# A hybrid attention, state-space and expert-retrieval block: low halves of gated tiles moved to ScalarE, low parts of expert blocks moved to VectorE, and a new order of issue

## The chip, the cores and the metric

The kernel runs on one core of a Trainium2 chip. The metric is the device time of one execution in microseconds; the median of several runs is compared. All engine times below are from one profiled execution.

## The reference

The input is a sequence of 512 tokens of width 1024, ahead of which 16 learned tokens are put. One layer is computed:

```python
proj = rms_norm(h, norm1_g) @ w_in
attn = sliding_window_attention(q, k, v)         # window 128, 8 query heads, 2 key heads, sinks
ssm  = s5_ssm(u)                                 # 32 groups, 64 complex states, then gelu and a gate
h = h + concat(rms_norm(attn), rms_norm(ssm)) @ w_out
# expert retrieval, 8 heads, on hc = rms_norm(h, norm2_g):
s1, s2 = q[..., :128] @ keys1.T, q[..., 128:] @ keys2.T          # q = hc @ w_query
sc, idx = top 16 of the sums of the top 16 of s1 and the top 16 of s2
act = gelu(hc @ u[idx]) * softmax(sc)
h = h + sum over the 16 picks of act * v[idx]    # 16384 experts, u and v are 16384 x 1024
```

## The kernel before, in words

**Mixer** (`front`): projections, state space, attention and the output product, up to the normalized activations hT, which lie transposed in SBUF as a high part hTh and a low part hTl. Products are taken in three passes, high by high, low by high and high by low; `split` makes the two parts of an operand (ScalarE rounds, VectorE subtracts). Its steps are written out in the table STEPS by name: Lx and Sx load and split x, Lwu, Lwq and Lwkv load weights and Swu, Swq, Swkv split them, u and q are the products with them, rot and co are GpSimd's rotations and output weights of the state space, and wt (L173, a helper that records every such operation) are its input weights on VectorE.

**Query and gate stages** (`body`, up to the end of the table WSTEPS). Steps, again by name:

- Lq, Aq, Dq, qm, qk, qs, qo: a block of w_query is loaded, rounded by ScalarE (Aq), its low part is subtracted (Dq, class `Query`, `lo`), multiplied and scored against the keys. tk and tp take the top 16; ca, ga, gx, gn, rk, xe and oh pick keys and gates of 128 tokens (class `Pick`).
- Lu, Au, Du, sm, so, each with a number b: an expert block of 128 experts is loaded into ur, rounded into uh on ScalarE, its low part ul is subtracted (`u_lo`), 24 matmuls give the scores of 384 tokens (`s_mm`), and ScalarE takes gelu (`s_out`). 51 blocks are done here ahead of the expert stage, in this order: by the table. ul and uh have two buffers each, and the query's parts share them.
- Class `Gates`: for the first three groups n of 128 tokens the gates are spread into a matrix over 128 x 128 experts. A tile holds 8 tokens: go makes the one-hot rows of both keys (goh), gg multiplies the second key's rows by the gate (ggt; the gate has a high half, elements 0 to 3 of the tile, and a low half, 4 to 7, both float16), gm multiplies the two on TensorE, four tokens at a time, gc copies the result into gst, and gs stores 16 tokens in DRAM. goh and ggt have two buffers each.
- rl and rs gather and use rows for the last 128 tokens, whose picks are fetched by themselves.

What is issued is a plain list: each step is recorded when its name comes up, and each engine runs its own instructions in that order. An instruction that waits holds up all that stand behind it on its engine. The names are in the tables; nothing else orders them.

**Expert stage** (the loop at the end of `body`): all gates are loaded from DRAM in turns (gc), and for each of 128 blocks the scores are multiplied by them (L1470), split (ph, pl) and multiplied with v (acc, 18 matmuls of 512 columns). For the blocks that were not done ahead, the steps of an expert block run there too, with the low part on VectorE.

The lines that the change touches:

```python
def gated(self, u):                                   # gg: both halves by VectorE
    ...
        self.nc.vector.tensor_tensor(g[:, qs], self.oh[u][:, 4:8], self.row(self.g2, u)[:, qs], op=ALU.mult)
(self.nc.vector if self.ct < 2 else self.nc.gpsimd).tensor_tensor(self.l, ...)          # Query.lo
(nc.gpsimd if b < AHEAD and b % LO[1] < LO[0] else V).tensor_tensor(lo, ...)            # u_lo, LO = (1, 1)
```

so that all 51 low parts of the blocks done ahead are GpSimd's, and of the query's 16 the first two VectorE's.

Of the kernel before, what the change touches and what calls it, by code (L numbers as in the profile page):

```python
# [1548 lines left out]
```

## Time and profile before

| | |
|---|---|
| time of three runs, median (lowest to highest) | 1556.37 us (1556.08 to 1556.42) |
| the profiled execution's own time, and its span | 1555.96 us, 1554.2 us |
| TensorE matmul busy, granted clock over the span | 1465.4 us (94%), 0.969 |
| TensorE weight load busy | 1293.8 us (83%) |
| VectorE busy | 1240.7 us (80%) |
| ScalarE busy | 639.9 us (41%) |
| GpSimd busy | 633.2 us (41%) |
| chain that ended last | TensorE 73%, VectorE 22% |

Busy time is the union of an engine's instructions as profiled; a matmul's end is modelled. The span is the time from the first to the last instruction. Idle time of an engine that is not the bound costs nothing. [...]

### The profile page before, as it was taken

How to read it: one execution, taken by the hardware profiler on the slowest of the kernel's cores; microseconds unless marked ns; L12 is line 12 of the kernel's file. 1: busy time of each engine (PE TensorE's matmuls, PEld its weight loads, DVE VectorE, ACT ScalarE, POOL GpSimd, SP SyncE). 2: the span in 40 equal slices, each digit the busy share in tenths (PEclk: the TensorE clock that was granted, in tenths of full speed). 3: DMA queues.
4: the chain of work that ended last, by engine and by line, in shares of the span. 5: the costliest groups of instructions: out<-in, count | busy, mean ns of one | idle time of the engine just before them, and what ended most of it. 6: DMA issues, size and time to landing. Idle time of an engine off the chain costs nothing.

```text
span 1554.2 us, 22068 instructions
## 1 busy us (share of the span) xinstructions
PE 1465.4 (94%) x8062; PEld 1293.8 (83%) x8062; DVE 1240.7 (80%) x2296; ACT 639.9 (41%) x995; POOL 633.2 (41%) x419
## 2 busy tenths in 40 slices
PE   7789898999788887999999999999999999999998
PEld 7667586889687787998879999999999999999886
DVE  8977934769999998847778887788878888778776
ACT  5235823334457665643333333333333333333332
POOL 6841210334454444552334444344434444344330
PEclk9779998999899898999999999999999999999999
DMA  6162116232456465786889999898998989999874
GB/s 235 59 93 75 62 41 239 92 112 76 144 188 234 158 232 184 255 314 216 291 300 351 327 356 349 314 327 304 339 318 311 344 290 344 311 318 335 307 271 149
DMA packets 161053, 371.60 MB, mean 239 GB/s; under 512 B 19872, under 2 KB 79008, under 8 KB 157744
## 3 DMA queue, kind: packets, MB, share of 16 engines
q1 hardware_dynamic: 123504, 234.90, 44.2%
q0 software_dynamic: 36864, 134.23, 24.5%
q8 instruction: 63, 1.03, 0.3%
q10 hardware_dynamic: 576, 1.05, 0.2%
q14 instruction: 46, 0.38, 0.1%
HBM read 330.91 MB, written 38.04 MB: 237 GB/s over the span
## 4 chain that ended last, share of the span: by engine, by line
PE 73%; DVE 22%; issue 2%; ACT 2%; DMA 1%; POOL 0%; SPq 0%; DVEq 0%; ACTq 0%
PE acc L1516 11%; PE acc L1517 11%; PE acc L1515 11%; PE ps_sb L1307 8%; PE ps_sb L1309 8%; PE ps_sb L1308 8%; DVE ggt L1190 5%; DVE goh L1180 3%; PE ps_qq L1045 2%; PE ps_qq L1046 2%; PE ps_qq L1047 2%; DVE wt L173 2%; DVE oh L1138 1%; PE ps_wo L186 1%; PE ps_wo L187 1%
## 5 line engine op out<-in xcount | busy, mean ns | idle before, releaser
L1307 PE MATMUL ps_sb<-hTh,uh 128*128 128x384 f32 x1024 | 353.4, 345 | 1.9 <-ACT uh L1295 1.9
L1309 PE MATMUL ps_sb<-hTh,ul 128*128 128x384 f32 x1024 | 348.3, 340 | 6.2 <-POOL ul L1299 5.5
L1308 PE MATMUL ps_sb<-hTl,uh 128*128 128x384 f32 x1024 | 346.8, 339 | 0.0
L1515 PE MATMUL acc<-vh,ph 128*128 128x512 f32 x768 | 299.5, 390 | 3.3 <-ACT ph L94 3.3
L1517 PE MATMUL acc<-vh,pl 128*128 128x512 f32 x768 | 301.3, 392 | 0.0
L1516 PE MATMUL acc<-vl,ph 128*128 128x512 f32 x768 | 301.0, 392 | 0.0
L1340 POOL DMA_INDIRECT row_grow<-in_v_rows_dram,idx x128 | 181.1, 1415 | 246.2 <-DVE ac L1367 194.9
L1340 POOL DMA_INDIRECT row_grow<-in_u_rows_dram,idx x116 | 158.1, 1363 | 249.9 <-DVE dots L1360 211.1
L1299 POOL TENSOR_TENSOR ul<-ur,uh 128x1024 fp32r<-128x1024 f32 x51 | 144.5, 2836 | 163.7 <-ACT uh L1295 163.5
L95 DVE TENSOR_TENSOR vl<-vr,vh 128x1024 fp32r<-128x1024 f32 x128 | 156.8, 1225 | 61.4 <-ACT vh L94 57.1
L1309 PEld LDWEIGHTS ps_sb<-hTh,ul 128*128 128x128 f32 x1024 | 194.9, 190 | 8.8 <-POOL ul L1299 7.8
L1307 PEld LDWEIGHTS ps_sb<-hTh,uh 128*128 128x128 f32 x1024 | 195.7, 191 | 5.6 <-ACT uh L1295 2.6
L1308 PEld LDWEIGHTS ps_sb<-hTl,uh 128*128 128x128 f32 x1024 | 195.7, 191 | 2.9
L1315 ACT ACTIVATE s<-ps_sb 128x384 f32<-128x384 f32 x128 | 63.0, 494 | 302.4 <-PE ps_sb L1309 299.2
L1367 DVE SCALAR_TENSOR_TENSOR ac<-row_grow,dots,ac 128x1024 f32<-128x1024 f32 x128 | 164.2, 1283 | 9.9 <-DMA row_grow<-in_v_rows_dram,idx 7.5
L1515 PEld LDWEIGHTS acc<-vh,ph 128*128 128x128 f32 x768 | 144.8, 189 | 32.2 <-ACT ph L94 3.9
L1517 PEld LDWEIGHTS acc<-vh,pl 128*128 128x128 f32 x768 | 144.5, 188 | 31.0 <-DVE pl L95 0.6
L1516 PEld LDWEIGHTS acc<-vl,ph 128*128 128x128 f32 x768 | 144.3, 188 | 28.4
L94 ACT CAST vh<-vr 128x1024 fp32r<-128x1024 f32 x128 | 134.0, 1047 | 40.3 <-PE acc L1517 38.4
L1295 ACT CAST uh<-ur 128x1024 fp32r<-128x1024 f32 x128 | 134.2, 1049 | 28.9 <-PE ps_sb L1308 9.6
L1360 DVE CUSTOM_DVE_ANT_0 row_grow<-row_grow,hcr 128x1024 f32<-128x1024 f32 x116 | 137.4, 1220 | 1.2 <-DMA row_grow<-in_u_rows_dram,idx 0.9
L94 ACT CAST ph<-s 128x384 fp32r<-128x384 f32 x100 | 51.4, 514 | 189.8 <-DVE s L1470 189.8
(338 smaller groups left out, 2331.4 us busy)
## 6 DMA issues: line engine op xcount, KB each, us to landing
ur<-in_uT_dram SPq DMA_DIRECT2D x128, 512.0 KB
vr<-in_v_dram SPq DMA_DIRECT2D x128, 512.0 KB
gates<-gst SPq DMA_DIRECT2D x24, 1024.0 KB
gc<-gates SPq DMA_DIRECT2D x16, 1536.0 KB
wqr<-in_w_query_dram SPq DMA_DIRECT2D x16, 512.0 KB
s_spill<-s SPq DMA_DIRECT2D x28, 192.0 KB
sr<-s_spill SPq DMA_DIRECT2D x28, 192.0 KB
wor<-in_w_out_dram SPq DMA_DIRECT2D x16, 256.0 KB
```

Source lines behind the costliest of these rows:

```text
L94: nc.scalar.copy(hi, src)
L95: (eng or nc.vector).tensor_tensor(lo, src, hi.bitcast(F32), op=ALU.subtract)
L1299: (nc.gpsimd if b < AHEAD and b % LO[1] < LO[0] else V).tensor_tensor(lo, ur.pop(b), hs[b].bitcast(F32), op=ALU.subtract)
L1307: E.matmul(p, hi[:, k], hTh[k][:, :384], start=(k == 0), stop=False)
L1308: E.matmul(p, hi[:, k], hTl[k][:, :384], start=False, stop=False)
L1309: E.matmul(p, lo[:, k], hTh[k][:, :384], start=False, stop=(k == KD - 1))
L1340: nc.gpsimd.indirect_dma_start(out=t, out_offset=None, in_=table, in_offset=bass.IndirectOffsetOnAxis(ap=idx[:, k:k + 1], axis=0))
L1360: V.tensor_tensor_reduce(t, t, hcr, 1.0, 0.0, op0=ALU.mult, op1=ALU.add, accum_out=dots[:, k:k + 1])
L1367: V.scalar_tensor_tensor(ac3, t, dots[:, k:k + 1], ac3, op0=ALU.mult, op1=ALU.add)
L1515: E.matmul(acc[n][h], ph[:, ts], vh[:, cs], start=(b == 0), stop=False)
L1516: E.matmul(acc[n][h], ph[:, ts], vl[:, cs], start=False, stop=False)
L1517: E.matmul(acc[n][h], pl[:, ts], vh[:, cs], start=False, stop=(b == 127))
```

## The change

It is in four parts. The new tables STEPS and WSTEPS hold the same steps as before in another order, and WSTEPS has new ones, gl. For the odd tiles u of each group (24 of 48), gg makes the high half alone, and gl makes the low half on ScalarE: two groups of four copies with a scale by partition, one copy for a token, reading and writing every second float16. The scale is the low part of the gate in float32 (gl). 28 of the 51 early low parts go to VectorE (the set UV), 23 remain on GpSimd. Of the query's low parts, VectorE has 0 and 7 in place of 0 and 1. The rest of the diff lets tiles be allocated in the new order (dictionaries in place of lists, views made only where they are used).

```diff
 STEPS = """
-    ang Lx0 Sx0 Lwu0 Lwu1 Swu0 Lwu3 Lwu4 sin Lwkv1 u0 Lx2 Lprm rot0 Swu3 Lx4 Sx1 par0 Swu1 par1 Swu4 par2 rot1
...
+    bdz Lx4 drz Lwu3 Lwu1 ang Lwu5 Lx0 Swu3 Sx4 Lwu0 Lwu4 Swu1 sin par0 Lprm Swu0 Sx1 Lwu6 Lwq0 par1 Sx0 Swu5 Lwkv3
...
+    wc01 q0 k1 wt20 us0 kv2 us3 wt21 Swq1 kvc0 we21 wt30 co20 wc11 kvc4 kvc1 q1 wt31 ui0 ui1 M0z kc1 we20 we31 we30
...
-        (self.nc.vector if self.ct < 2 else self.nc.gpsimd).tensor_tensor(self.l, self.raw, self.h.bitcast(F32), op=ALU.subtract)
+        (self.nc.vector if self.ct in QV else self.nc.gpsimd).tensor_tensor(self.l, self.raw, self.h.bitcast(F32), op=ALU.subtract)
...
+        self.gl = GP.tile([128, 128], F32, name=f"gl{n}", tag="gl", bufs=2)
         g8 = gT.rearrange("p (u t) -> p u t", t=8)
-        V.tensor_copy(self.g2[:, :, 0], g8)
-        V.tensor_tensor(self.g2[:, :, 1], g8, self.g2[:, :, 0], op=ALU.subtract)
+        V.tensor_copy(self.g2[:, 0], g8)
+        V.tensor_tensor(self.gl.rearrange("p (u t) -> p u t", t=8), g8, self.g2[:, 0], op=ALU.subtract)
+        V.tensor_copy(self.g2[:, 1], self.gl.rearrange("p (u t) -> p u t", t=8))
...
     def gated(self, u):
-        self.g[u] = g = self.GP.tile([128, 8, 128, 2], F16, name="ggt", tag="ggt", bufs=2)
-        for x in range(2):
-            qs = slice(4 * x, 4 * x + 4)
-            self.nc.vector.tensor_tensor(g[:, qs], self.oh[u][:, 4:8], self.row(self.g2, u)[:, qs], op=ALU.mult)
+        for x in range(1 if u in LA[self.n] else 2):
+            self.nc.vector.tensor_tensor(self.out(u)[:, 4 * x:4 * x + 4], self.oh[u][:, 4:8],
+                                         self.row(self.g2[:, x, u], 4), op=ALU.mult)
+
+    def gated_low(self, u, q):
+        oh, g = self.oh[u], self.out(u)
+        for x in range(4 * q, 4 * q + 4):
+            y, s = divmod(x, 2)
+            t = u * 8 + x
+            self.nc.scalar.activation(g[:, 4 + y, :, s], oh[:, 4 + y, :, s], AF.Copy, scale=self.gl[:, t:t + 1])
...
+QV = {0, 7}
+LA = [{u for u in range(16) if u % 2}] * 3
+UV = {0, 2, 4, 5, 6, 8, 10, 11, 15, 16, 17, 19, 20, 22, 29, 32, 36, 37, 38, 39, 40, 41, 43, 46, 47, 48, 49, 50}
...
-    gc2.7.0 sm8 gc2.7.1 Lu9 gc2.6.1 so8 gs2.3 Au12 sm17 so17 Du12 Au9 sm12 rl11 Au7 Du9 Du7 Lu18 sm9 so12 Au18 so9
-    sm7 Du18 so7 rs11 sm18 so18
+    gc2.15.0 gg2.6 gs2.6 so17 Du12 gn3 gc2.14.0 rs9 gc2.7.0 rl7 gm2.7.1 gm2.6.1 rs7 gc2.7.1 Lu18 gm2.6.0 gs2.7 gc2.6.1
+    Au7 Du9 gc2.6.0 sm12 sm9 Du7 so12 rs10 rl8 so9 Au18 Du18 gs2.3 sm7 sm18 so7 so18 rs8
 """
...
-            (nc.gpsimd if b < AHEAD and b % LO[1] < LO[0] else V).tensor_tensor(lo, ur.pop(b), hs[b].bitcast(F32),
+            (nc.gpsimd if b < AHEAD and b not in UV else V).tensor_tensor(lo, ur.pop(b), hs[b].bitcast(F32),
                                                                                 op=ALU.subtract)
...
+                            if u in LA[n]:
+                                step(f"gl{n}.{u}.{q}", g.gated_low, u, q)
                             step(f"gm{n}.{u}.{q}", g.mm, u, q)
```

How it stands in the order, at two places. VectorE, the first gated tiles of the first group of tokens, before (goh one-hot, ggt gated; a line of x2 is the two halves of one tile):

```order
L1180 TENSOR_TENSOR goh_4133<-itx_2502,iT0_4122 128x2048
L1190 TENSOR_TENSOR ggt_4163<-goh_4133,g20_4126 128x1024 x2
L1180 TENSOR_TENSOR goh_4166<-itx_2502,iT0_4122 128x2048
L1432 SCALAR_TENSOR_TENSOR idx_2485<-i1_2482,i2_2483 128x128
L1190 TENSOR_TENSOR ggt_4195<-goh_4166,g20_4126 128x1024 x2
```

and now, on VectorE:

```order
L1182 TENSOR_TENSOR goh_4217<-itx_2502,iT0_4130 128x2048
L1196 TENSOR_TENSOR ggt_4219<-goh_4217,g20_4134 128x1024
L1182 TENSOR_TENSOR goh_4221<-itx_2502,iT0_4130 128x2048
L1196 TENSOR_TENSOR ggt_4258<-goh_4221,g20_4134 128x1024 x2
L1319 TENSOR_TENSOR ul38_4261<-ur38_3259,uh38_4202 128x1024
```

An odd tile has one VectorE operation in place of two, and a low part (ul38) stands among them.

ScalarE, at the end of the gate stage, before (gst copies gate results from PSUM, uh rounds an expert block, s is gelu of a block's scores, vh belongs to the expert stage):

```order
L1295 CAST uh17_6664<-ur17_6629 128x1024
L1205 COPY gst_6647<-ps_gm_6677 128x4x128
L1205 COPY gst_6647<-ps_gm_6666 128x4x128
L1205 COPY gst_6647<-ps_gm_6649 128x4x128
L1315 ACTIVATE s8_6716<-ps_sb8_6687 128x384
L1295 CAST uh12_6719<-ur12_6598 128x1024
L1315 ACTIVATE s17_6746<-ps_sb17_6721 128x384
L1295 CAST uh9_6750<-ur9_6713 128x1024
L94 CAST vh0_6899<-vr0_6893 128x1024
L1295 CAST uh7_6779<-ur7_6662 128x1024
```

and now:

```order
L1315 CAST uh9_6869<-ur9_6687 128x1024
L1219 COPY gst_6718<-ps_gm_6725 128x4x128
L1335 ACTIVATE s17_6878<-ps_sb17_6830 128x384
L1219 COPY gst_6718<-ps_gm_6807 128x4x128
L1219 COPY gst_6888<-ps_gm_6855 128x4x128
L1219 COPY gst_6888<-ps_gm_6892 128x4x128
L1219 COPY gst_6888<-ps_gm_6901 128x4x128
L1315 CAST uh7_6925<-ur7_6871 128x1024
L1219 COPY gst_6888<-ps_gm_6914 128x4x128
L1335 ACTIVATE s12_6982<-ps_sb12_6930 128x384
```

The last copy of gates now stands behind uh7 and ahead of blocks 12, 9, 7 and 18; before, it stood ahead of blocks 8, 17, 12, 9, 7 and 18. uh7 takes the buffer of uh12, two roundings back, which block 12's matmuls read; on TensorE these stand behind the last gate matmul.

## Rows read from the trace of the kernel before

**Rows 1.** Busy time of each engine in stretches of the execution: the stretch in us from the span's start, its length, then for PE, PEld (weight loads), DVE, ACT and POOL the busy us and the count of instructions, the granted clock, the busy share of the DMA engines, and GB/s.

```profile
0.00:256.70 256.70, 222.54 (x1397) 175.99 (x1397) 198.95 (x404) 116.89 (x312) 98.69 (x98) 0.92 0.39 107
...
41.00:129.00 88.00, 75.87 (x519) 58.68 (x520) 75.69 (x103) 28.01 (x62) 50.85 (x33) 0.81 0.46 87
...
250.00:275.00 25.00, 20.21 (x81) 16.49 (x82) 10.84 (x46) 8.07 (x22) 5.00 (x3) 0.80 0.66 231
...
256.70:369.90 113.20, 112.47 (x550) 95.06 (x551) 77.29 (x516) 35.59 (x50) 39.63 (x17) 0.98 0.31 107
...
300.00:325.00 25.00, 25.00 (x126) 21.05 (x125) 18.06 (x124) 8.37 (x12) 9.45 (x5) 1.00 0.28 95
...
369.90:666.60 296.70, 252.37 (x1808) 240.50 (x1807) 279.64 (x545) 173.45 (x206) 142.55 (x55) 0.93 0.56 198
```

**Rows 2.** Who waited for whom, TensorE in 369.9 to 694.2 us: the instruction and what ended the wait, us in total, times, the longest.

```profile
PE ps_gm L1199 <- DVE ggt L1190: 14.8, 17, 2.9
...
PE ps_gm L1198 <- DVE ggt L1190: 12.6, 11, 2.8
```

**Rows 3.** The same for ScalarE in 369.9 to 666.6 us.

```profile
ACT s L1315 <- PE ps_sb L1309: 37.7, 17, 5.8
...
ACT gst L1205 <- PE ps_gm L1199: 35.9, 16, 7.1
```

**Rows 4.** Groups of VectorE's instructions of one shape in 369.9 to 666.6 us: line, operation, out<-in, shape, count | busy us, mean ns of one | idle us just before them and what ended it.

```profile
L1190 DVE TENSOR_TENSOR ggt<-goh,g 128x1024 f16<-128x1024 f16 x96 | 100.3, 1093 | 0.8
...
L1180 DVE TENSOR_TENSOR goh<-itx,iT 128x2048 f16<-128x2048 f16 x48 | 63.1, 1330 | 12.0 <-PE ps_gm L1199 12.0
...
L1132 DVE TENSOR_TENSOR oh<-it,rk 128x2048 f16<-128x2048 f16 x8 | 14.8, 1847 | 0.1
...
L1135 DVE TENSOR_TENSOR oh<-oh,xe 128x2048 f16<-128x2048 f16 x8 | 13.8, 1720 | 0.4
...
L1138 DVE TENSOR_TENSOR oh<-oh 128x1024 f16<-128x1024 f16 x8 | 11.8, 1474 | 0.2
```

**Rows 5.** Single operations on VectorE over the whole execution: duration in ns, shortest/median/longest, first and last start.

```profile
L1190 DVE TENSOR_TENSOR ggt<-goh,g x96: 674/685/3232, 429.1 to 665.8; 128x1024 f16<-128x1024 f16 x96
...
L1180 DVE TENSOR_TENSOR goh<-itx,iT x48: 1203/1217/3443, 427.8 to 654.3; 128x2048 f16<-128x2048 f16 x48
...
L1299 DVE TENSOR_TENSOR ul<-ur,uh x77: 1220/1226/1227, 813.0 to 1438.9; 128x1024 fp32r<-128x1024 f32 x77
```

**Rows 6.** VectorE in order of time: start us, us, engine, line, operation, out<-in, shape, count. Both handle 128 integers.

```profile
449.82 2.28 DVE L1111 TENSOR_SCALAR tci<-tci 128x128 uint32<-128x128 uint32 x1
...
454.39 0.21 DVE L1115 CAST tc<-tci 128x128 f32<-128x128 uint32 x1
```

**Rows 7.** GpSimd in order of time, the same columns, and the idle time before with what ended it.

```profile
446.35 8.03 POOL L1299 TENSOR_TENSOR ul<-ur,uh 128x1024 fp32r<-128x1024 f32 x2 [6.83 <-ACT uh L1295]
```

**Rows 8.** GpSimd's group of low parts in 369.9 to 666.6 us, columns as in rows 4.

```profile
L1299 POOL TENSOR_TENSOR ul<-ur,uh 128x1024 fp32r<-128x1024 f32 x44 | 127.5, 2902 | 149.3 <-ACT uh L1295 149.2
```

**Rows 9.** ScalarE in order of time in the mixer; L448 is a copy of 128 x 128 from SBUF with a scale by partition, and the second row is the instruction right behind it.

```profile
47.91 0.39 ACT L448 ACTIVATE dg<-ident,r 128x128 f32<-128x128 f32 x1
...
48.20 0.39 ACT L587 COPY bdr<-prm 64x256 f32<-64x256 f32 x1
```

**Rows 10.** Groups of ScalarE's instructions of one shape in 240 to 860 us, columns as in rows 4; ACT_TABLE_LOAD loads the table of an activation function.

```profile
L1205 ACT COPY gst<-ps_gm 128x512 f32<-128x512 f32 x96 | 92.9, 1096 | 41.7 <-PE ps_gm L1199 35.9 <-issue 5.6
...
L1052 ACT COPY qqT<-ps_qq 128x512 f32<-128x512 f32 x16 | 9.4, 585 | 39.7 <-PE ps_qq L1047 39.7
...
L1315 ACT ACT_TABLE_LOAD x4 | 5.1, 1283 | 0.1
```

**Rows 11.** ScalarE in order of time at the hand-over, with the idle time before and what ended it; a row of L1315 follows the end of one block's 24 matmuls, L1295 is a rounding uh.

```profile
667.95 2.86 ACT L1205 COPY gst<-ps_gm 128x512 f32<-128x512 f32 x3
...
671.85 0.49 ACT L1315 ACTIVATE s<-ps_sb 128x384 f32<-128x384 f32 x1 [1.04 <-PE ps_sb L1309]
...
672.23 1.04 ACT L1295 CAST uh<-ur 128x1024 fp32r<-128x1024 f32 x1
...
676.05 0.49 ACT L1315 ACTIVATE s<-ps_sb 128x384 f32<-128x384 f32 x1 [2.77 <-PE ps_sb L1309]
```

**Rows 12.** TensorE in order of time: the first of the last 32 gate matmuls (four groups), the first matmul behind them, and the first of the expert stage.

```profile
665.09 0.23 PE L1198 MATMUL ps_gm<-ggt,goh 128*128 128x128 f16 x1
...
667.36 0.42 PE L1307 MATMUL ps_sb<-hTh,uh 128*128 128x384 f32 x1
...
694.14 0.39 PE L1515 MATMUL acc<-vh,ph 128*128 128x512 f32 x1
```

**Rows 13.** VectorE's waits in 369.9 to 666.6 us, columns as in rows 2.

```profile
DVE goh L1180 <- PE ps_gm L1199: 12.0, 6, 3.1
```

**Rows 14.** DMA issues on SyncE's queue, in order of time: the last store of gates and the first load.

```profile
670.83 0.33 SPq L1209 DMA_DIRECT2D gates<-gst  x1
...
676.20 0.38 SPq L1460 DMA_DIRECT2D gc<-gates  x1
```

**Rows 15.** VectorE in order of time at the hand-over: the product of scores and gates of block 0, and the low part pl made from it.

```profile
688.80 1.38 DVE L1470 SCALAR_TENSOR_TENSOR s<-gc,s 128x384 f32<-128x384 f32 x1 [1.30 <-DMA gc<-gates]
...
690.75 0.56 DVE L95 TENSOR_TENSOR pl<-s,ph 128x384 fp32r<-128x384 f32 x1 [0.58 <-ACT ph L94]
```

**Rows 16.** One kind of the mixer's wt on VectorE, columns as in rows 5.

```profile
L173 DVE TENSOR_TENSOR wt<-prm,pr x8: 667/1796/1919, 41.2 to 80.9; 128x512 f32<-128x512 f32 x8
```

More of the change, by code (lines that the diff above doesn't have):

```diff
@@ L317, in params @@
         def params(i):
-            prm = t["prm"]
-            b_re, b_im, c_re, c_im, bbr, bbi, tb1, tb2 = (prm[:, x] for x in range(8))
+            if i >= 4:
+                b_re, b_im, c_re, c_im, bbr, bbi, tb1, tb2 = (t["prm"][:, x] for x in range(8))
             if i == 0:
@@ new lines, in row, with out @@
+    def row(self, z, n):
+        return z.rearrange("p (q s) -> p q s", s=2)[:, :, None].to_broadcast([128, n, 128, 2])
+    def out(self, u):
+        if u not in self.g:
+            self.g[u] = self.GP.tile([128, 8, 128, 2], F16, name="ggt", tag="ggt", bufs=2)
+        return self.g[u]
+    def gated(self, u):
+        for x in range(1 if u in LA[self.n] else 2):
+            self.nc.vector.tensor_tensor(self.out(u)[:, 4 * x:4 * x + 4], self.oh[u][:, 4:8],
+                                         self.row(self.g2[:, x, u], 4), op=ALU.mult)
@@ L1201, in copy @@
     def copy(self, u, q):
-        if u % 2 == 0 and q == 0:
+        if u // 2 not in self.st:
             self.st[u // 2] = self.GP.tile([128, 128, TS], F32, name="gst", tag="gst", bufs=2)
@@ new lines @@
+    oh2.1.3 go1.12 oh2.1.4 go1.13 gl1.15.0 gl1.15.1 so0 gc1.5.1 gc1.4.0 gg1.12 Lu20 gm1.14.0 gm1.15.1 gs1.3 so3 Au6
+    gm1.14.1 oh2.1.5 gc1.14.0 Du6 gm1.15.0 sm4 go1.10 gc1.4.1 gm1.12.0 gl1.13.0 gs1.2 gc1.15.0 gt2 gg1.13 Lu14 gp2
+    Lu13 gc1.15.1 gg1.10 gm1.12.1 Au11 Du11 sm6 gc1.14.1 gm1.13.0 gl1.13.1 go2.0 gc1.12.1 so6 gc1.13.0 gm1.13.1
+    gc1.13.1 go2.1 gs1.7 gg2.0 gc1.12.0 gm1.10.1 gm1.10.0 so4 gg2.1 gs1.6 go1.11 go2.5 Au13 gl2.1.1 sm11 gg1.11
+    gm2.1.1 gg2.5 gm2.0.1 gm2.0.0 Au14 gl2.1.0 go2.4 Du13 gm2.1.0 rl6 gc2.1.1 gl1.11.0 go2.2 gl2.5.1 gc2.0.0 sm13
@@ new lines @@
+    gl2.5.0 gg2.4 Du14 Lu10 gc2.0.1 gg2.2 gc1.10.1 Lu19 Lu5 gl1.11.1 so13 gm2.5.1 gc2.1.0 so11 gm2.5.0 gm1.11.0
+    gm1.11.1 sm14 Au20 gm2.4.0 gc1.11.0 gc1.11.1 Du20 go2.8 gs2.0 gc1.10.0 so14 gc2.5.0 Au10 gm2.4.1 Lu16 rs6 go2.9
+    gg2.8 gm2.2.0 Du10 gc2.4.0 go2.3 gm2.2.1 gc2.5.1 sm20 gl2.9.0 gg2.9 gc2.4.1 Lu22 rl4 rl5 Au16 so20 gl2.9.1 gm2.8.1
+    gs1.5 gl2.3.0 Au5 rl3 gm2.8.0 sm10 gg2.3 gs2.2 Du16 gm2.9.0 gm2.9.1 go2.10 so10 gc2.8.1 gc2.9.0 Lu21 Du5 gc2.8.0
+    Au19 sm16 gg2.10 rs4 rl11 Lu2 gm2.10.1 Du19 so16 gc2.9.1 gm2.10.0 go2.11 gm2.3.0 gl2.3.1 gl2.11.1 gl2.11.0 rs3
@@ new lines @@
+    gg2.11 Au21 gs2.4 gc2.2.0 sm5 gm2.3.1 gc2.2.1 go2.13 sm19 so5 gl2.13.1 go2.12 gg2.13 gc2.3.0 gm2.11.1 Au2 rs5
+    gg2.12 gc2.3.1 Du21 gm2.11.0 gc2.11.1 Du2 go2.15 so19 Lu15 sm21 Au15 Du15 gm2.13.1 gc2.10.0 gm2.12.0 so21 gg2.15
+    gc2.10.1 gm2.12.1 gc2.11.0 Au22 rs11 sm2 Lu8 sm15 gl2.13.0 gl2.15.0 gl2.15.1 so2 Du22 Lu17 Lu9 gc2.13.1 go2.14
+    gs2.1 gm2.13.0 Au8 gm2.15.1 gg2.14 gc2.13.0 gc2.15.1 gs2.5 so15 Du8 gm2.15.0 go2.7 rl9 gl2.7.1 Au17 Lu12 sm22
+    gc2.12.1 rl10 so22 gc2.12.0 sm8 gl2.7.0 gm2.14.0 Au12 Du17 gg2.7 gm2.14.1 sm17 gm2.7.0 gc2.14.1 so8 go2.6 Au9 Lu7
```

138 lines of the change are left out of this document (61 added, 77 removed).

## The prediction

> **What bounds the kernel now.** I read the page's engine totals first, then busy times by stretch, then who waited for whom in the stretch that the change is about, then single operations there. The stretches [rows 1]: mixer 0 to 257 us, query stage 257 to 370, gate stage 370 to 667 (from the first candidate sums, ca3, to the last gated tile, gg2.6), hand-over 667 to 694, and expert stage from 694 to the end, where TensorE is full. The gate stage is 296.7 us long and VectorE is busy for 279.6 of it; TensorE is busy for 252.4 at a granted clock of 0.93, ScalarE for 173.5. So VectorE sets the pace there: TensorE's largest waits are 27.4 us for gated tiles [rows 2]. ScalarE is often idle there, for PE's results (37.7 and 35.9 us) [rows 3].
>
> VectorE's own operations are not at one length. A gated half has a median of 685 ns and a mean of 1093; a one-hot tile 1217 and 1330 [rows 4, 5]. The long ones stand beside GpSimd's subtractions: two of these ran in 446 to 454 us, and a shift of 128 integers took 2.28 us there where a conversion of as many took 0.21 right after [rows 6, 7]. A GpSimd subtraction thus stops VectorE for about 2 us. Over the stage, mean minus median of like operations is 39 us for 96 gated halves, 5 for 48 one-hots, 9 for 16 oh of 2048 (L1132, L1135, against the one-hot's 1217) and 6 for 8 oh of 1024 (against 685): 60 us in these forms alone beside 44 subtractions [rows 4, 5, 8], so 1.4 us for one at least; the single case says 2.1. I take 1.8.
>
> **The change, part by part.** *Low parts of 28 blocks on VectorE.* Of the 44 GpSimd subtractions in the gate stage 18 are left. VectorE gains 26 x 1.8 = 47 us of waits and pays 28 x 1.226 us (its own time for this operation [rows 5]) = 34 us: net -13 us. With 1.4 it is -2, with 2.1 it is -21. The query's two on VectorE remain two (0 and 7 for 0 and 1), at nothing: TensorE is full in that stage [rows 1].
>
> *Low halves of the odd tiles on ScalarE.* 24 of 96 gated halves leave VectorE, 24 x 0.685 = -16 us. ScalarE gets 192 scaled copies of 128 x 128. The nearest rows are the mixer's dg, the same form from SBUF with a scale by partition: 0.39 to 0.40 us long, 0.29 to 0.31 from one start to the next [rows 9]. 192 x 0.31 = 60 us. No row shows a copy whose elements lie 4 bytes apart on both sides. ScalarE's gst copy, which writes with a step, takes 1.096 us for 512 elements, while qqT, packed, takes 0.585 [rows 10]: 1.87 times as long for as many, so the upper end is 0.58 and the lower 0.29. I take 0.31, the nearer form. Two more table loads stand in the new order, 1.28 us each [rows 10].
>
> [...]
>
> *Gate stage.* VectorE: 279.6 - 16 - 13 = 250. ScalarE: 173.5 + 60 + 3 = 236. TensorE at full clock: 46 blocks of 4.2 us (one result each 4.20 us [rows 11]) and 93 groups of gate matmuls of 0.5 (32 matmuls, four groups, in 2.3 us [rows 12]), 240 (before, 44 blocks: 232). VectorE remains the longest, but the three now lie within 14 us, each in a fixed order, and each odd tile has one more station (VectorE, ScalarE, TensorE), held up by whatever ScalarE waits for. Before, the stage was VectorE's 280 + 17, of which 12.0 us were waits for gate matmuls to free a one-hot buffer [rows 13]. I put the new idle time at 22 us: stage 272, a gain of 25. The bounds: 250 + 10 = 260 where less stalling also gives TensorE its clock back, and 290 where ScalarE's waits (123 us idle before) shrink by little more than half: 236 + 54.
>
> *Hand-over.* Before, the last gate matmul ended at 667.4, the last gst copies at 670.8, the store went out at 670.8, the load of gates at 676.2, VectorE had them at 688.8 and ph and pl by 691.3; TensorE was busy with six blocks until 694.1 and never waited for them [rows 11, 12, 14, 15]. In the new order four blocks (12, 9, 7, 18) stand behind the last gate matmul, 16.8 us. And the last gst copy stands behind uh7 on ScalarE, whose buffer is free only when block 12's matmuls are done: 4.2 + 1.04 + 0.95 us after the last gate matmul, 6.2 instead of 3.4 [rows 11, 12]. From there the chain is as before, 691.3 - 670.8 = 20.5. So the first expert matmul starts 26.7 us after the last gate matmul, about 28 us after the last gated tile, and TensorE stands idle for 10 us. Before it was 27.6 after the last gated tile, so this costs 0.5, and the clock after the pause more: where TensorE stood idle for 4.8 us in 250 to 275, the clock was 0.80 for those 25 us [rows 1]. That is 10 us at the lower level, at most 5 us of work; I take 3. Together +3.5. Lower end 0; upper 8, where the load is late too.
>
> *Mixer.* No work is added there; the loads and the splits of w_u, the transposes wt, and q0 and q1 change places. Two q steps (24 matmuls at 25.0 / 126 = 0.20 us [rows 1], 4.8 us) move from behind the last wt to ahead of it, where TensorE has room. But wt itself is held by GpSimd: of its 24 operations the eight of one kind have a median of 1.80 us and a shortest of 0.67 [rows 16], and GpSimd is busy for 50.9 of the 88 us between 41 and 129 [rows 1]. The order moves that, it doesn't remove it. I take -3, from -12 to +8: the first w_u product now has to wait for more loads and splits, with VectorE as the bound (75.7 of 88 us between 41 and 129 [rows 1]).
>
> *Expert stage.* Untouched, 694 to 1554.
>
> **Sum**, against the profiled execution's own 1555.96 us (0.4 below the median of the runs, 1556.37): -25 + 3.5 - 3 = -24.5, so 1531.5; with the 0.4 for the median, 1532.
>
> **The rivals.**
> 1. *The freed VectorE time is mostly not used.* TensorE and ScalarE, in fixed orders, become the bound, and the stage ends at 285: 1532 + 13 = 1545. For it: three engines within 14 us of each other. Against it: before, VectorE was idle for only 17 us of 297 and TensorE and ScalarE followed it. Chance 0.22.
> 2. *More than forecast.* A subtraction is worth 2.1 us, and with fewer stalls TensorE keeps its clock: stage 255 to 260, mixer -6: 1514. For it: the single case of 2.1 us, and the clock of 0.93. Chance 0.20.
> 3. *ScalarE becomes the bound, slower than before.* The price of one scaled copy decides. ScalarE's stage is 176 + 192 p plus the idle time of a pacing engine, 17 to 20 us as VectorE had. At p = 0.53 us that is 297, the old length. At the upper end, 0.58, it is 307: 1532 + 35 = 1567. [...] Against it: dg's 0.31, and that gst's step is 64 bytes and not 4. Chance 0.08.
> 4. *VectorE's long operations are not GpSimd's doing*, or GpSimd's row gathers cost the same; then the 34 us are added and only 16 leave: 1556 + 18 + 1 = 1575. The shift of 2.28 us speaks against it [rows 6, 7]. Chance 0.03.
>
> **How the numbers follow.** The forecast has 0.47, its own range 1521 to 1543. The range reaches from 1511 (rival 2) to 1554 (rival 1 with a late hand-over). A measurement of this kernel can tell about 0.2% from no change: 1553.3 to 1559.5. Rivals 3 and 4 lie above (slower 0.11); of rival 1, 0.04 lies within, a stage of 290 with a mixer that loses; the rest is faster, 0.85.
>
> **What would show it.** Right: the gate stage at about 272 us, VectorE busy 250 and gated halves with a mean below 0.95 us; 18 GpSimd subtractions in it; scaled copies 0.4 us long, ScalarE busy about 236; a pause of 10 us of TensorE ahead of the first expert matmul, with a granted clock below 1 behind it; mixer and query within a few us of 370. Wrong: scaled copies above 0.5 us, one-hots waiting far more than 12 us for gate matmuls, a mixer longer by 8 us or more.

## The result, and the profile after

The changed kernel takes 1522.38 us (median of 4 runs, 1521.88 to 1522.85), the kernel before, beside it, 1556.39 (1556.08 to 1558.8): a ratio of 0.9778, 95% interval 0.9761 to 0.9795, 34 us faster. The forecast was 1532, range 1511 to 1554. The profiled execution of the changed kernel took 1522.77 us, its span is 1520.7.

The page's engine totals of the changed kernel, busy us, share of the span and instructions:

```profile
PE 1453.0 (96%) x8062; PEld 1285.6 (85%) x8062; DVE 1188.1 (78%) x2303; ACT 692.9 (46%) x1189; POOL 545.1 (36%) x391
```

Its stretches, cut at the same events as those of before [rows 1], columns as there: mixer, query stage, gate stage, hand-over, and the first 25 us from the first acc matmul.

```profile
0.00:254.00 254.00, 218.89 (x1397) 175.67 (x1398) 189.16 (x403) 115.18 (x311) 97.95 (x98) 0.94 0.38 106
254.00:367.10 113.10, 112.42 (x550) 94.36 (x551) 80.29 (x517) 36.35 (x51) 39.68 (x17) 0.98 0.34 112
367.10:627.87 260.77, 248.00 (x1849) 237.53 (x1848) 231.96 (x545) 228.04 (x401) 60.26 (x29) 0.98 0.64 222
627.87:656.10 28.23, 18.24 (x120) 17.91 (x117) 9.27 (x13) 11.61 (x16) 13.31 (x9) 0.91 0.91 328
656.10:681.10 25.00, 24.98 (x99) 20.43 (x100) 13.56 (x19) 8.87 (x11) 0.36 (x1) 0.89 0.64 217
```

Against the spans of before, 1554.2 - 1520.7 = 33.5 us, stretch by stretch:

| us | before | forecast | after |
|---|---|---|---|
| mixer | 256.7 | -3 | 254.0 (-2.7) |
| query stage | 113.2 | 0 | 113.1 (-0.1) |
| gate stage | 296.7 | -25 | 260.8 (-35.9) |
| hand-over | 27.5 | +0.5 | 28.2 (+0.7) |
| expert stage, to the end of the span | 860.1 | +3 | 864.6 (+4.5) |

So nearly all of the surprise is in the gate stage. There TensorE is now the longest, 248.0 of 260.8 at a granted clock of 0.98 (the share of TensorE's full speed that was granted), ScalarE follows with 228.0, and VectorE has gone from 279.6 to 232.0. VectorE's and GpSimd's groups there that answer to [rows 4] and [rows 8], columns as there:

```profile
L1196 DVE TENSOR_TENSOR ggt<-goh,g 128x1024 f16<-128x1024 f16 x72 | 53.1, 777 | 0.3
L1182 DVE TENSOR_TENSOR goh<-itx,iT 128x2048 f16<-128x2048 f16 x48 | 58.0, 1224 | 21.0 <-PE ps_gm L1213 20.8
L1135 DVE TENSOR_TENSOR oh<-oh,xe 128x2048 f16<-128x2048 f16 x8 | 9.8, 1220 | 0.2
L1132 DVE TENSOR_TENSOR oh<-it,rk 128x2048 f16<-128x2048 f16 x8 | 9.8, 1220 | 0.1
L1319 DVE TENSOR_TENSOR ul<-ur,uh 128x1024 fp32r<-128x1024 f32 x28 | 34.2, 1220 | 5.7 <-ACT uh L1315 5.7
L1319 POOL TENSOR_TENSOR ul<-ur,uh 128x1024 fp32r<-128x1024 f32 x18 | 44.3, 2463 | 103.8 <-ACT uh L1315 75.9 <-DVE ggt L1196 27.9
```

The forms that were long are short: a gated half has a mean of 777 ns instead of 1093, an oh of 2048 elements 1220 instead of 1847. I summed, over all VectorE operations of the gate stage, what each took beyond the shortest of its line and names: 84.3 us before, 21.6 after, so 62.7 us less. The forecast had 47.

Part of this is the 26 subtractions that left; the rest is where the others stand. Experiment 4 gives the new order alone, with all 43 that begin in the stage still on GpSimd, 67.8 us in place of 84.3. GpSimd and VectorE in order of time, changed kernel, first at 391.9 us and then at 624.3 us:

```profile
391.90 4.72 POOL L1319 TENSOR_TENSOR ul<-ur,uh 128x1024 fp32r<-128x1024 f32 x2 [4.82 <-ACT uh L1315]
```

```profile
392.02 0.23 DVE L1015 MATCH_REPLACE8 cand<-tsc,cand 128x80 f32<-128x80 f32 x1
...
392.38 0.38 DVE L1017 MAX8 tsc<-cand 128x8 f32<-128x80 f32 x2
...
392.73 0.23 DVE L1019 FIND_INDEX8 tci<-tsc,cand 128x8 uint32<-128x80 f32 x1
...
624.38 3.49 DVE L1196 TENSOR_TENSOR ggt<-goh,g 128x1024 f16<-128x1024 f16 x2
```

```profile
624.31 2.41 POOL L1319 TENSOR_TENSOR ul<-ur,uh 128x1024 fp32r<-128x1024 f32 x1 [5.88 <-ACT uh L1315]
```

The top-16 operations (MAX8, FIND_INDEX8, MATCH_REPLACE8) take 0.23 us, or 0.38 for two in a row, beside two subtractions, as elsewhere in this execution (medians of 0.23 to 0.24 us over 32 of each, none above 0.25); the pair of gated halves beside the last one takes 3.49 us instead of 1.3. A subtraction thus costs VectorE about 2.2 us where an operation of two tiles begins beside it (1.9 to 2.2 in five places of this stage; 0.3 to 0.9 us in three places where the first such operation begins late in it), and 0.1 to 0.2 us where only the top-16's stand beside it. An operation with one tile as input was not always free: before the change the shift of [rows 6] (2.28 us, where the median of its four is 0.23), and the conversion right behind it (2.45 us, median 0.22), ran beside the two subtractions of [rows 7] and were held up as well:

```profile
452.02 2.45 DVE L1114 CAST tr<-ri 128x128 f32<-128x128 uint32 x1
```

The hand-over of the changed kernel, rows that answer to [rows 11, 12, 14, 15]: ScalarE's last copy of gates, the load of gates on SyncE's queue, VectorE's first product and TensorE's first matmul of the expert stage.

```profile
634.33 1.05 ACT L1219 COPY gst<-ps_gm 128x512 f32<-128x512 f32 x1
```

```profile
641.12 0.37 SPq L1482 DMA_DIRECT2D gc<-gates  x1
```

```profile
654.97 0.56 DVE L1492 SCALAR_TENSOR_TENSOR s<-gc,s 128x384 f32<-128x384 f32 x1 [8.30 <-DMA gc<-gates]
```

```profile
656.12 0.79 PE L1537 MATMUL acc<-vh,ph 128*128 128x512 f32 x1 [10.02 <-ACT ph L94]
```

TensorE's pause is 10.02 us, the chain from the last copy (635.4) to the first matmul 20.7 us, and the granted clock over the next 25 us is 0.89, all three about as forecast.

### The profile page after: what moved, and what is told of

It reads as the page before. It is cut to its first block, busy times and chain, and to the rows that moved or that the text cites. A ratio compares the mean times of both kernels' runs of the same rounds, so it can differ in the third digit from the quotient of the medians.

```text
span 1520.7 us, 22245 instructions
## 1 busy us (share of the span) xinstructions
PE 1453.0 (96%) x8062; PEld 1285.6 (85%) x8062; DVE 1188.1 (78%) x2303; ACT 692.9 (46%) x1189; POOL 545.1 (36%) x391
## 4 chain that ended last, share of the span: by engine, by line
PE 71%; issue 8%; POOL 6%; ACT 6%; DVE 5%; DMA 3%; SPq 1%; POOLq 0%; ACTq 0%; DVEq 0%
PE acc L1537 9%; PE acc L1538 9%; PE acc L1539 9%; PE ps_sb L1327 9%; PE ps_sb L1329 8%; PE ps_sb L1328 8%; POOL row_grow L1360 2%; POOL ptmp L172 2%; PE ps_qq L1045 2%; PE ps_qq L1047 2%; PE ps_qq L1046 2%; ACT gst L1219 2%; ACT ggt L1204 1%; DMA row_grow<-in_v_rows_dram,idx 1%; ACT uh L1315 1%
## 5 line engine op out<-in xcount | busy, mean ns | idle before, releaser
L1360 POOL DMA_INDIRECT row_grow<-in_v_rows_dram,idx x128 | 180.4, 1410 | 248.0 <-DVE ac L1387 190.7
L1538 PEld LDWEIGHTS acc<-vl,ph 128*128 128x128 f32 x768 | 145.5, 189 | 27.4
L1319 DVE TENSOR_TENSOR ul<-ur,uh 128x1024 fp32r<-128x1024 f32 x105 | 128.5, 1224 | 35.5 <-ACT uh L1315 35.5
L1315 ACT CAST uh<-ur 128x1024 fp32r<-128x1024 f32 x128 | 134.8, 1054 | 19.3 <-PE ps_sb L1328 6.8
L1380 DVE CUSTOM_DVE_ANT_0 row_grow<-row_grow,hcr 128x1024 f32<-128x1024 f32 x116 | 137.5, 1220 | 1.9 <-DMA row_grow<-in_u_rows_dram,idx 1.9
```

Source lines behind the costliest of these rows:

```text
L1315: S.copy(hs[b], ur[b])
L1360: nc.gpsimd.indirect_dma_start(out=t, out_offset=None, in_=table, in_offset=bass.IndirectOffsetOnAxis(ap=idx[:, k:k + 1], axis=0))
L1380: V.tensor_tensor_reduce(t, t, hcr, 1.0, 0.0, op0=ALU.mult, op1=ALU.add, accum_out=dots[:, k:k + 1])
L1538: E.matmul(acc[n][h], ph[:, ts], vl[:, cs], start=False, stop=False)
```

## The experiments

All times are medians of 4 to 8 runs, with the ratio to the kernel before, run beside it on the same chip (1555.4 to 1557.0 us). Gate stages are cut as above. Where low parts go back to GpSimd, blocks 16 and 40 stay on VectorE: in the new order, row gathers that stand ahead of their low parts on GpSimd wait for buffers that these give back.

**1. The same number of low parts on VectorE, other blocks (uv_swap).**

```diff
-UV = {0, 2, 4, 5, 6, 8, 10, 11, 15, 16, 17, 19, 20, 22, 29, 32, 36, 37, 38, 39, 40, 41, 43, 46, 47, 48, 49, 50}
+UV = {1, 3, 5, 8, 14, 15, 16, 17, 19, 24, 25, 26, 27, 29, 30, 31, 32, 33, 34, 35, 36, 37, 40, 42, 44, 47, 49, 50}
```

> 28 of the 51 early low parts stay on VectorE, but 14 are exchanged: those of blocks 1, 3, 14, 24 to 27, 30, 31, 33, 34, 35, 42, 44 go to VectorE, and those of 0, 2, 4, 6, 10, 11, 20, 22, 38, 39, 41, 43, 46, 48, which stand among one-hots and gated halves, go to GpSimd. Theory N (a GpSimd subtraction costs VectorE about 2.2 us where a two-input operation of VectorE begins beside it, and some 0.2 where only the top-16 operations stand beside it): the excess of VectorE's operations over their shortest, 21.6 us in the gate stage of the changed kernel, rises by about 14 x 1.8 = 25 to some 45, VectorE busy from 232 to about 256, time 1535 to 1545. Rival C (each subtraction costs the same, wherever it stands): excess 17 to 26 as before, time 1520 to 1526. Rival P (TensorE paces the stage now and VectorE has room): the excess rises as in N, time 1522 to 1528.

Measured: 1581.05 us, ratio 1.0142 (1.0111 to 1.0173), 26 us above the kernel before (1555.4 beside it). VectorE's excess is 38.9 us instead of 21.6 (45 expected), of which 30.9 stand beside the 18 subtractions (14.5 in the changed kernel): N is right in kind against C. But that is 17 us, VectorE's busy time rose by 16 to 248.1, and the stage by 60 to 320.6. The gate stage (columns as in [rows 1]), TensorE's waits there, and VectorE's (instruction and what ended the wait, us in total, times, longest):

```profile
370.60:691.20 320.60, 263.26 (x1849) 249.01 (x1848) 248.10 (x545) 229.74 (x401) 63.37 (x29) 0.91 0.52 181
...
PE ps_sb L1329 <- DVE ul L1319: 39.2, 10, 8.6
PE ps_gm L1212 <- DVE ggt L1196: 8.0, 6, 2.4
...
DVE goh L1182 <- PE ps_gm L1213: 49.0, 21, 6.0
DVE ul L1319 <- ACT uh L1315: 16.2, 8, 4.9
```

In the changed kernel TensorE waits for low parts on VectorE for 1.3 us, for gated tiles for 2.3, and VectorE's one-hots wait for 20.8. Of the stage's 60 us, 38 are thus TensorE's waits for low parts, 8 those for gated tiles, and 15 its longer busy time, 263.3 us at a granted clock of 0.91 in place of 248.0 at 0.98. In the two longest of the ten waits for a low part (8.6 and 6.5 us) VectorE was mostly at top-16 operations that stand ahead of it; in three others, 13.8 us together, the low part itself was held up beside a subtraction on GpSimd. One of these, 3.38 us long where the mean in the changed kernel is 1.22, VectorE and GpSimd in order of time:

```profile
463.10 3.38 DVE L1319 TENSOR_TENSOR ul<-ur,uh 128x1024 fp32r<-128x1024 f32 x1
...
462.75 2.64 POOL L1319 TENSOR_TENSOR ul<-ur,uh 128x1024 fp32r<-128x1024 f32 x1 [12.59 <-ACT uh L1315]
```

TensorE, in order, stands still for a late low part (39.2 us in ten waits), and the gate matmuls behind that block come late; that this is why VectorE's one-hots wait more is read from the order and not shown by itself. No theory of mine had priced these waits.

**2 to 4. Undoing a part, in the new order (uv_two, la_none, order_only).** The low parts, the low halves, and both:

```diff
-UV = {0, 2, 4, 5, 6, 8, 10, 11, 15, 16, ...}     # uv_two, order_only
+UV = {16, 40}
-LA = [{u for u in range(16) if u % 2}] * 3       # la_none, order_only; the steps gl leave the table
+LA = [set()] * 3
```

> 26 of the 28 low parts back on GpSimd (all but blocks 16 and 40, which the order of row loads wants on VectorE); low halves of odd tiles stay on ScalarE. Theory N or C: VectorE loses 26 x 1.22 = 32 us of its own and gains 26 x 2.2 = 57 us of stalls: busy about 257 in the gate stage, time about 1540 to 1547. The forecast's price of 1.8 us would give 47 - 32 = 15: 1532 to 1537. Rival P (TensorE paces): 1522 to 1528.

> All low halves of gated tiles back on VectorE, 24 more operations of 0.685 us, and no scaled copies on ScalarE; low parts and order as changed. If VectorE paces the stage: + 16 us, 1536 to 1540. Rival P (TensorE paces it, VectorE sat idle for 29 us): 1522 to 1528. If the scaled copies had cost TensorE or VectorE waits of their own: faster than 1520.

> Both parts undone but the order kept: low halves on VectorE, 49 of 51 low parts on GpSimd. If the two parts make the gain and add up: 232 + 16 + 25 = 273 us of VectorE in the gate stage, stage about 295, time 1553 to 1560, the kernel before less the mixer's 3 us. If the new order by itself is worth something (it sets which operations stand beside a GpSimd subtraction): below 1548.

**5 to 7. Each part, and both, in the order of before (before_uv, before_la, before_both).** Both tables and QV as before; the copies gl, where they are, right behind the tile's gated half:

```diff
-    ... gg0.9 gc0.1.0 gm0.9.1 ...
+    ... gg0.9 gl0.9.0 gl0.9.1 gc0.1.0 gm0.9.1 ...    # before_la, before_both, each odd tile
```

> The order of before (mixer and gate stage) and all low halves of gated tiles on VectorE, as before; only the 28 low parts of the change go from GpSimd to VectorE. Theory S (each part pays by itself: VectorE loses the stalls and pays 28 x 1.22 us): of 43 subtractions in the gate stage of before, which cost 95 us of stalls, some 26 leave with about 58, VectorE gains 24 to 28 us, time 1528 to 1536. Theory T (a part pays only in an order made for it: low parts on VectorE stand behind what VectorE does or waits for, and TensorE waits for them, as in uv_swap, where these waits were 39 us): 1545 to 1575.

> The order of before with only the low halves of the odd tiles on ScalarE, their copies put right behind the tile's high half in the list. Theory S: VectorE loses 24 x 0.685 = 16 us, time 1538 to 1546. Theory T (the copies stand behind what ScalarE waits for there, TensorE gets odd tiles later): 1552 to 1575.

> The order of before with both parts: 28 low parts on VectorE and low halves of the odd tiles on ScalarE. Theory S: the two gains add, 1514 to 1528, the whole gain without the new order. Theory T: 1535 to 1565, so that the new order is worth the rest, 13 us or more.

Measured, 2 to 7 together, medians in us with the ratio to before and its interval:

| order | neither part | low parts only | low halves only | both |
|---|---|---|---|---|
| of before | 1 (before) | 1542.9, 0.990 (0.987 to 0.994) | 1581.3, 1.016 (1.012 to 1.019) | 1571.1, 1.009 (1.006 to 1.011) |
| new | 1573.6, 1.010 (1.006 to 1.013) | 1528.7, 0.983 (0.980 to 0.986) | 1568.7, 1.007 (1.005 to 1.010) | 1522.4, 0.978 (0.976 to 0.980) |

The column "low halves only" of the new order is uv_two. None of the six came out in a range that was named for it: before_uv lies between S and T, before_la and before_both above T, order_only and uv_two above all that was named, la_none just above P.

In either order the two parts add up with each other: -14 and +24 make 10 in the order of before (14 measured), -45 and -5 make -50 in the new one (-51). What does not add up is the order with the parts. By itself the new order loses 18 us, and with both parts it gains 49 (1571.1 to 1522.4); the low parts are worth 14 us in the order of before and 45 in the new one, and the low halves lose 24 in the order of before and gain 5 to 6 in the new one. Theory T is right in kind, with one exception: the low parts pay by themselves too, by about half of what S gave. The order of before was tried with one place for the copies, right behind the tile; another place was not.

The gate stage by stretch, of order_only, la_none and before_uv, columns as in [rows 1]:

```profile
369.10:680.10 311.00, 259.00 (x1847) 244.13 (x1846) 262.40 (x543) 176.66 (x209) 128.06 (x55) 0.94 0.54 185
```

```profile
363.50:634.50 271.00, 250.88 (x1848) 238.86 (x1848) 248.22 (x569) 176.67 (x209) 62.07 (x29) 0.97 0.62 214
```

```profile
371.40:654.60 283.20, 244.06 (x1786) 232.03 (x1785) 261.11 (x575) 172.00 (x204) 60.27 (x28) 0.96 0.59 207
```

All eight, in the gate stage, us:

| | before | before_uv | before_la | before_both | order_only | la_none | uv_two | changed |
|---|---|---|---|---|---|---|---|---|
| stage | 296.7 | 283.2 | 316.8 | 308.9 | 311.0 | 271.0 | 306.0 | 260.8 |
| VectorE busy | 279.6 | 261.1 | 256.7 | 244.5 | 262.4 | 248.2 | 241.3 | 232.0 |
| VectorE idle | 17.1 | 22.1 | 60.1 | 64.4 | 48.6 | 22.8 | 64.7 | 28.8 |

Each step can be compared four ways. The low parts take 9 to 19 us off VectorE's busy time, the low halves 16 to 23, the new order 12 to 17. The idle time has no such value for a step: it goes from 17 to 49 with the order alone, and from 65 to 29 with the low parts behind it. VectorE was busy for 35 us less in before_both than before, and the stage was 12 us longer. In order_only and la_none the waits behind the idle time are these, first order_only, then la_none, columns as above:

```profile
PE ps_sb L1325 <- POOL ul L1315: 17.3, 6, 11.2
...
DVE goh L1182 <- PE ps_gm L1213: 44.5, 18, 14.9
```

```profile
PE ps_sb L1325 <- POOL ul L1315: 2.9, 2, 1.4
...
DVE goh L1182 <- PE ps_gm L1213: 16.4, 13, 4.0
```

The new order counts on low parts that are ready soon; from GpSimd, where they can stand behind a row gather that waits itself, they aren't, and TensorE waits. The longest of these waits in order_only, 11.2 us, is of this kind, on GpSimd in order of time:

```profile
538.42 0.96 POOL L1356 DMA_INDIRECT row_raw<-in_u_rows_dram,idx  x1 [18.60 <-DVE dots L1376]
539.40 4.67 POOL L1315 TENSOR_TENSOR ul<-ur,uh 128x1024 fp32r<-128x1024 f32 x2
```

In before_la it is ScalarE that waits most, for one-hots, with copies of gates and gelu behind it:

```profile
ACT ggt L1205 <- DVE goh L1183: 28.3, 10, 6.3
```

In the changed kernel this is 0.8 us.

**8. The mixer's order of before (old_mixer).** The table STEPS alone goes back:

```diff
-STEPS = """ bdz Lx4 drz Lwu3 Lwu1 ang ...
+STEPS = """ ang Lx0 Sx0 Lwu0 Lwu1 Swu0 ...
```

> The changed kernel with the mixer's order of before (the table STEPS); query, gate and expert stages as changed. If the mixer's order is worth the 2.8 us that the two profiles show: 1524 to 1527. If those 2.8 us are the scatter of one execution (five executions with the new mixer began the query stage between 250.5 and 257.0 us): 1519 to 1524.

Measured: 1525.05 us (1524.49 to 1525.19), ratio 0.9792 (0.9765 to 0.9819). The interval overlaps the changed kernel's, so the ratios don't separate them. The profiles do better: in nine executions with the new mixer the first query matmul starts at 253.9 us on average (250.4 to 257.6), in five with the old one at 256.9 (255.0 to 258.2). The means differ by 3.0 us with a standard error of 1.0, so the gain is most likely the new order's, though one execution alone could not have shown it.

**9. Four more low parts on VectorE (uv_more).**

```diff
+UV |= {1, 3, 12, 14}
```

> The changed kernel with four more low parts on VectorE, those of blocks 1, 3, 12 and 14, whose subtractions on GpSimd (513.4, 527.9, 624.3 and 558.5 us) each still stop a VectorE operation for 2.0 to 2.2 us. Theory N (the neighbours set the price): 4 x 2.17 = 8.7 us of stalls leave, 4 x 1.22 = 4.9 come, VectorE busy from 232 to 228; time 1518 to 1522, the last gated tile 2 us earlier in any case (block 12 stands beside it). Theory W (what decides is where the low part stands in the order that TensorE waits through): 1521 to 1530, with waits of TensorE for ul on VectorE above the 1.3 us of the changed kernel.

Measured: 1529.57 us, ratio 0.9846 (0.9803 to 0.9889). VectorE's busy time fell by 5.0 to 227.0, somewhat more than N gave, and the stage grew by 13 to 273.5: TensorE waits 9.1 us for VectorE's low parts (1.3 in the changed kernel) and VectorE 38.2 for gate matmuls (20.8). W is right. Taking work from the engine that is stopped made the stage longer.

**10 to 12. The hand-over (gc_split, tail_split, loads_order).** The first load of gates in two pieces; then a shorter end of the gate stage as well; then the loads in the order of need:

```diff
-                G.dma_start(gcs[b // BC], gd[:, :, b:b + BC]...)
+                for x, y in ((0, 2), (2, BC)) if b == 0 else ((0, BC),):               # gc_split, tail_split
+                    G.dma_start(gcs[b // BC][:, :, x:y], gd[:, :, b + x:b + y]...)
+                for x, y in ((0, 2),) if b == 0 else ((0, BC),):                       # loads_order
...
-    ... so17 Du12 gn3 gc2.14.0 rs9 gc2.7.0 rl7 gm2.7.1 gm2.6.1 rs7 gc2.7.1 Lu18 gm2.6.0 gs2.7 gc2.6.1
-    Au7 Du9 gc2.6.0 sm12 sm9 Du7 so12 rs10 rl8 so9 Au18 Du18 gs2.3 sm7 ...
+    ... so17 Du12 gc2.14.0 gc2.7.0 gm2.7.1 gm2.6.1 gc2.6.1 gn3 rs9 rl7 rs7 gc2.7.1 gm2.6.0 gs2.7
+    gc2.6.0 gs2.3 Lu18 Au7 Du9 sm12 sm9 Du7 so12 rs10 rl8 so9 Au18 Du18 sm7 ...       # tail_split, loads_order
+UV |= {12}                                       # and gc2.7.0, gc2.6.1 on VectorE
...
                 v_load(b + 2)                                                          # loads_order
+                if b == 0:
+                    G.dma_start(gcs[0][:, :, 2:], gd[:, :, 2:BC]...)                   # the second piece here
-                while loads >= 1:
+                for _ in range(min(int(loads), 3) if b >= 2 else 0):                   # row gathers from block 2 on
```

> The changed kernel with the first load of gates in two pieces, that of blocks 0 and 1 first and that of blocks 2 to 7 behind it; nothing else. If the pause of 10 us ahead of the first expert matmul hangs on the chain last copy, store, load (641.1 to 655.0 us), multiply: the load of a quarter of the bytes lands 5 to 9 us earlier, the pause shrinks to 1 to 5 us, and the time by as much and 1 to 3 us more for the clock: 1511 to 1518. If the load waits for something else (other transfers in the queues, the store's landing): 1520 to 1524.

> As gc_split, and the end of the gate stage shortened as well: block 12's low part on VectorE (its subtraction on GpSimd stops the last gated half for 2.2 us), the last copy of gates and its store ahead of uh7 and of the load of block 18, and two of the last six copies of gates on VectorE, which is idle there. The last store goes out 3 to 6 us earlier. If the pause is the chain's: it is gone, the time 3 to 6 us below gc_split's as far as there is pause left: 1508 to 1515. If another wait sets the first expert matmul (blocks 9, 7 and 18, their loads): no more than gc_split.

> As tail_split, with the loads of the hand-over in the order in which they are needed: the first piece of the gates, then v of block 1, then v of block 2, then the second piece; and the row gathers of the first two expert blocks put off (then three a block at most until they have caught up). If the hand-over is bound by transfers that go ahead of those that are needed (in gc_split and tail_split the pause came back one block later, 7.3 and 6.1 us, for v of block 1): both pauses shrink to 0 to 4 us together and the time to 1508 to 1516. If the bytes alone bind it, or the put-off gathers come back later in the expert stage: 1517 to 1524.

Measured: gc_split 1523.94 us, ratio 0.9785 (0.9747 to 0.9823), no gain over the changed kernel. The first expert matmul came after 2.88 us of waiting instead of 10.02, but the next block then waited 7.33, in TensorE's order of time:

```profile
651.62 0.50 PE L1538 MATMUL acc<-vh,ph 128*128 128x512 f32 x1 [2.88 <-ACT ph L94]
663.48 0.80 PE L1538 MATMUL acc<-vh,ph 128*128 128x512 f32 x1 [7.33 <-ACT ph L94]
```

What was late there is v of block 1, on ScalarE; its load stands behind both pieces of the gates on SyncE's queue:

```profile
643.66 4.03 SPq L1483 DMA_DIRECT2D gc<-gates  x2
647.79 10.60 SPq L1477 DMA_DIRECT2D vr<-in_v_dram  x5
...
660.11 1.04 ACT L94 CAST vh<-vr 128x1024 fp32r<-128x1024 f32 x1 [8.15 <-DMA vr<-in_v_dram]
```

tail_split: 1520.65 us, ratio 0.9769 (0.9735 to 0.9803), the same story, with one wait of 6.1 us. loads_order: 1511.69 us (1511.16 to 1515.79), ratio 0.9712 (0.9686 to 0.9738), 10.7 us below the changed kernel, with its gate stage no shorter than tail_split's (259.8 us in both). Both pauses are gone but for 1.2 us, and the clock over the whole span is 0.986 instead of 0.978. TensorE's first expert matmuls, and the expert stage of tail_split and of loads_order:

```profile
647.39 0.50 PE L1542 MATMUL acc<-vh,ph 128*128 128x512 f32 x1 [0.17 <-ACT ph L94]
657.03 0.50 PE L1542 MATMUL acc<-vh,ph 128*128 128x512 f32 x1 [1.04 <-ACT ph L94]
...
652.98:1522.90 869.92, 855.13 (x4152) 759.47 (x4152) 677.21 (x829) 302.00 (x413) 335.15 (x240) 0.99 0.87 308
...
647.39:1509.10 861.71, 852.35 (x4152) 757.50 (x4152) 677.68 (x829) 302.07 (x413) 334.70 (x240) 1.00 0.88 311
```

So the pause is a matter of which transfers go first at a time when the DMA engines are 0.91 busy, and it and the low clock behind it cost 8 to 9 us (8.2 in the expert stage, 9.0 between the medians 1511.69 and 1520.65, on two chips whose kernel before differs by 1.1). This version beats both kernels. Which of its two edits (the order of the loads, the gathers put off) does more was not tried.

## Why the prediction was right, and where it was off

- **The bound.** VectorE's long operations were GpSimd's doing, as the forecast said; rival 4 falls with the rows at 391.9 and 624.3 us. VectorE paced the stage before; it no longer does: TensorE is busy for 248.0 of 260.8 us (240 forecast) and waits for gated tiles for 2.3 us instead of 27.4 [rows 2]. The 240 were low by a rounding: four groups of gate matmuls in 2.3 us [rows 12] are 0.57 us each and not 0.5, which gives 246.
- **The low halves.** The term of -16 us is VectorE's -16.2 between la_none and the changed kernel. The scaled copies are 0.42 to 0.53 us long, four in 1.30, and 192 of them 62.3 us: the nearer row, 0.31, was the right one to take (60 forecast), and rival 3 falls. The stage is 10.2 us shorter by this part (271.0 to 260.8) and not 16, as VectorE's idle time grew by 6; between the medians it is 6 us (between the two profiled spans 5.7, as la_none's mixer was 3.5 us shorter in its execution). A half takes ScalarE 2.6 us, eight copies, and VectorE 0.685, but that price does not decide here: ScalarE had the time (busy for 228.0 of 260.8 us, and TensorE waited for gated tiles for 2.3).

```profile
L1204 ACT ACTIVATE ggt<-goh,gl 128x128 f16<-128x128 f16 x192 | 62.3, 459 | 0.9 <-DVE goh L1182 0.8
```

- **The low parts.** The forecast took one price for each subtraction, 1.8 us, and a net of -13 us for VectorE. Taking 26 or 27 of them from GpSimd lowers the excess by 38 to 50 us in the four comparisons, 1.5 to 1.9 each, and VectorE's busy time by 14.2 (order_only to la_none), 9 to 19 over all four. So the term was about right as a mean. As a price of one it is not: of the 43 that begin within the stage before, 34 have 2 us or more of excess beside them, and of the 17 that begin within it now, 12 have under 1 us, ten of these beside the top-16.
- **The order, put at nothing.** The forecast gave the new order of the gate stage no term of its own. It takes 17.2 us off VectorE's busy time from before to order_only, where the stage's subtractions are still on GpSimd (12 to 17 in the four comparisons); the excess falls by nearly as much, 84.3 to 67.8, since other operations stand beside them. On this path -17.2 for the order, -14.2 for the low parts, -16.2 for the low halves and +11.7 of idle time make the stage's -35.9. With both parts in place the order also brings VectorE's idle time from 64 to 29 us; that was read from the waits, and no run takes the order apart.
- **The idle time.** 22 us were forecast for VectorE, 28.8 measured, mostly one-hots that wait for gate matmuls (20.8, 12.0 before [rows 13]). Nothing in the forecast said that this needs an order that suits these 28 blocks; with 28 others in the same order it was 72.5. The forecast, a sum of busy times plus one idle time for all, gives uv_swap about 1538 (248.1 + 28.8, 16 us more than the changed kernel) and order_only about 1553; they took 1581 and 1574. That the total came within 10 us is in part luck: the term of 17 us that was left out is offset by 7 us of idle time and by 2 us behind the stage. Rival 2 (stage 255 to 260) came nearest to the stage's 260.8 and had the clock of 0.98 right, but not the cause: its price of 2.1 us is above the 1.5 to 1.9 measured, and the mixer did not bring its -6.
- **The hand-over.** Right in its steps: the last copy 6.2 us after the last gate matmul, 20.7 us from there to the first expert matmul (20.5 forecast), 10 us of pause, low clock behind it. The clock cost 2.9 us there (3 forecast): 99 matmuls in the first 25 us in place of 112, at 0.22 us each. TensorE ran them at a granted clock of 0.50 for 5.4 us, the same lower level as in the kernel before in 251.6 to 261.8 us, within the stretch that the forecast was read from. The expert stage is 4.5 us longer in all; the rest lies in its last 40.7 us, where the granted clock was 0.89, before 0.96, for which nothing was forecast and no cause was sought. First the changed kernel, twice, then before, twice:

```profile
656.10:661.50 5.40, 5.38 (x13) 4.22 (x14) 2.81 (x4) 1.56 (x2) 0.00 (x0) 0.50 0.85 323
...
1480.00:1520.70 40.70, 32.71 (x133) 26.18 (x131) 24.52 (x31) 9.80 (x13) 2.39 (x2) 0.89 0.41 143
...
1513.50:1554.20 40.70, 33.34 (x139) 26.60 (x137) 25.88 (x32) 9.80 (x13) 3.62 (x2) 0.96 0.42 152
...
251.60:261.80 10.20, 7.01 (x20) 5.58 (x21) 5.86 (x16) 3.43 (x10) 0.00 (x0) 0.50 1.02 373
```

- **The mixer.** -2.7 for a forecast of -3, borne out by the mean of 14 executions, not by one.

## What to carry to other kernels

An operation that holds up another engine had no price of its own here (a subtraction on GpSimd cost VectorE 0.1 to 2.2 us by what began beside it): read which operations begin beside each instance, before the change and after it, and sum those. A new order of issue is a part of the change like the others and needs a term of its own, since it sets those neighbours (-17.2 us of VectorE's busy time in order_only). Where engines run in fixed orders and wait for one another, a part is worth what its place in the order lets it be worth (the low parts 14 us in the order of before, 45 in the new one); a sum of busy times predicts busy times, and the waits have to be read for one order and one assignment together. A pause at a change of stage can be a queue that carries the later need ahead of the earlier one: splitting the load alone gave nothing (gc_split 1523.94 us against 1522.38), and with the piece that is needed next going next, and the gathers put off, the time fell by 9 us (1520.65 to 1511.69).
